# First piece of weights in two halves, compression's weights loaded at another place, residual pairs inside priority blocks, two squares left to TensorE

## The chip, the cores and the metric

One core of one Trainium2 chip runs the whole program; the other cores are idle. The metric is the device time of one execution in microseconds (us). TensorE (PE) multiplies, VectorE (DVE) and ScalarE (ACT) do the elementwise work, SyncE (SP) issues the transfers from memory, GpSimd (POOL) does almost nothing.

## The reference

256 positions of width 1024 in float32 go through a first part of two layers and a second part of two layers. Each layer of the first part has three kinds of attention side by side (one of them with a compressed branch: blocks of 32 keys and values go through a small network with the weights `cw1` and `cw2`), cross attention to a memory of 256 rows, and a gated feed-forward with a short convolution. The second part has a retention layer and a convolution layer, each followed by a feed-forward, with scales, shifts and gates that come from a condition vector:

```python
hx = hx + g1 * yx                                   # yx: retention or convolution mixer
fx = modulate(rms_norm_2(hx, norm_ffn[i]), sh2, sc2)
hx = hx + g2 * swiglu(fx, ffn_w1[i], ffn_w3[i], ffn_w2[i])
...
return rms_norm_2(hx, final_norm)
```

The kernel returns the 256 x 1024 result of the last norm.

## The kernel before, in words

**Numbers in three products.** Every float32 weight `w` is split into a coarse part `wh` (a cast on ScalarE, line 378) and a rest `wl` (a subtraction on VectorE, line 379), every activation likewise into `xh` and `xl`. A product is three matmuls on TensorE: `wh,xh`, `wh,xl`, `wl,xh` (helper `mm`, line 297).

**Weights.** `Stream` (line 344) brings the weights in pieces of 128 x 1024 numbers (512 KB; some are a little smaller) in the order in which the program asks for them: SP issues the transfer into one of five `raw` buffers, ScalarE and VectorE split it into one of four pairs `wh`, `wl`. A buffer pair comes free with the last matmul that reads it.

**Activations.** `X` holds the 8 tiles (k = 0 to 7) of 128 channels by 256 positions. Two tiles are a pair. `residual_pair` (line 750) adds a finished bank `o` to a pair of X, `split_gain` makes `xh` and `xl` of its two tiles for the next layer, and `Norm.pair` squares the pair on ScalarE and adds the squares into `ss` on VectorE. `Norm.totals` adds the two halves and lets PE sum over the channels; `rsqrt` makes the norm's factor of it (`rx` to `ry` in the rows). A factor is put to use after the matmuls of the next layer, so the next layer's matmuls start with `xh` and `xl` and not with the norm. With `late`, the last pair's square isn't added into `ss`: PE sums it by itself.

**Residuals of the second part.** `residual` (line 1580) calls `residual_pair(os_(p), p, ...)` for the four pairs. It is called four times: after the retention, after the first feed-forward, after the convolution mixer, after the second feed-forward. In three of them `os_(p)` returns a bank that is finished already (`accs[p]`). At the convolution's output `os_(p)` is `fm(bxs)` (line 487): it asks for two pieces of weights and issues the 48 matmuls of that pair. In the rows of before the four banks there are `mm_16337`, `mm_16406`, `mm_16476`, `mm_16546`.

**Memory and compression.** In each layer of the first part `mem_pair` (line 791) splits the memory's rows from the tile `memx`, loaded in two halves into one buffer with the tag `big4`. The same buffer then takes the compression's first weights in two halves (`load_w1`, line 800; the tile is `w1`, in the trace `w`), called in `compress` (line 895) just before the matmuls that read each half.

**What sets the order.** A scheduler orders each engine's instructions by a priority, which is the place in the program, and by when their inputs are there in its own reckoning. `tc.high_priority(offset=n)` moves what stands in the block ahead by n places and sets the place back on leaving the block to where it was on entering it. `PRIO` is 300.

Of the kernel before, what the change touches and what calls it, by code (L numbers as in the profile page):

```python
# [10 lines left out]
F32 = mybir.dt.float32  # L11
# [3 lines left out]
AF = mybir.ActivationFunctionType  # L15
ALU = mybir.AluOpType
# [258 lines left out]
def tile_two_blocks(ctx, tc, aps, out):  # L275
    nc = tc.nc
    W, X_IN, MEM_IN, CTX_IN = aps["w"], aps["x"], aps["mem"], aps["ctx"]
# [24 lines left out]
    def tt(out, a, b, op):  # L302
        V.tensor_tensor(out=out, in0=a, in1=b, op=op)  # L303
# [10 lines left out]
    def act(out, a, func, scale=1.0, bias=None, accum_out=None):  # L314
        kw = {}
        if bias is not None:
            kw["bias"] = bias
        if accum_out is not None:
            kw["accum_out"] = accum_out
        A.activation(out=out, in_=a, func=func, scale=scale, **kw)  # L320
# [23 lines left out]
    class Stream:  # L344
# [12 lines left out]
        def dma(s):  # L357
            i = s.n_dma
            if i >= len(_PLAN) or i >= s.n_split + s.nraw:
                return  # L360
            t = wraw_p.tile([128, 1024], F32, tag="raw", name="raw", bufs=s.nraw)
            b, first = i // _PER, (i // _PER) * _PER
            n = _SIZES[i]
            o = sum(_SIZES[first:i]) * 128
            nc.sync.dma_start(out=t[:, :n], in_=W[b][o:o + 128 * n].rearrange("(p n) -> p n", p=128))
            s.raw[i] = t, n
            s.n_dma += 1

        def split(s):
            i = s.n_split  # L370
            if i >= s.n_dma:
                return False
            pools, bufs, ids = s.rings[int(i < s.until and i % 2)]
            if len(ids) >= bufs and ids[-bufs] >= (s.n_get - 1 if s.hold is None else s.hold):
                return False
            t, n = s.raw.pop(i)
            h, l = (p.tile([128, 1024], F32R, tag=a, name=a, bufs=bufs, at=128) for p, a in zip(pools, ("wh", "wl")))
            act(h[:, :n], t[:, :n], AF.Copy)
            tt(l[:, :n], t[:, :n], h[:, :n].bitcast(F32), ALU.subtract)
            ids.append(i)  # L380
            s.parts[i] = h, l, n
            s.n_split += 1
            s.dma()
            return True
# [156 lines left out]
    PRIO = 300  # L541
# [9 lines left out]
    class Norm:  # L551


        def __init__(s, gains=None, tags=("a0", "a1"), late=False):
            s.ss, s.last = None, None
            s.gains = gains
            s.tags = tags
            s.late = late
            s.prio = PRIO

        def pair(s, p, src=None, ps=None):
            src = X if src is None else src
            ps = p if ps is None else ps
            tag = "ss" if s.ss is None else "sq"
            sq = rot_p.tile([128, 2, T], F32, tag=tag, name=tag)
            if s.gains is None:
                act(sq, src[:, 2 * ps:2 * ps + 2, :], AF.Square)
            else:
                for e in range(2):
                    k = 2 * p + e  # L570
                    act(sq[:, e, :], src[:, k, :], AF.Square, scale=s.gains[:, k:k + 1])
            if s.ss is None:
                s.ss = sq
            elif p == 3 and s.late:
                s.last = sq
            else:
                tt(s.ss, s.ss, sq, ALU.add)

# [4 lines left out]

        def totals(s):
            s.ps = bank(s.tags[0])
            parts = [s.ss] if s.last is None else [s.ss, s.last]
            for a, part in enumerate(parts):
                tt(part[:, 0, :], part[:, 0, :], part[:, 1, :], ALU.add)
                for t in range(2):
                    mm(s.ps[:, t:t + 1], part[:, 0, t * 128:(t + 1) * 128], ones[:, 0:1], start=a == t == 0, stop=True)  # L590
# [65 lines left out]
    nrm, xs = Norm(), xs_tiles()  # L656
# [93 lines left out]
    def residual_pair(o, p, gain, nrm, xs, g=None):  # L750
        xv = X[:, 2 * p:2 * p + 2, :]
        if g is None:
            tt(xv, xv, o.rearrange("p (n t) -> p n t", n=2), ALU.add)
        else:
            for e in range(2):
                k = 2 * p + e
                stt(X[:, k, :], o[:, e * T:(e + 1) * T], g[:, k:k + 1], X[:, k, :], ALU.mult, ALU.add)
        if gain is not None:
            for k in (2 * p, 2 * p + 1):
                split_gain(xs, X, k, gain)  # L760
        nrm.pair(p)
# [15 lines left out]
    def layer(i, xs, nrm, last_gain, background=None, second=None):  # L777
        with ExitStack() as es:
# [10 lines left out]
            memx = {}  # L789

            def mem_pair(p):
                if p % 2 == 0:
                    memx["t"] = cp.tile([128, 4, T], F32, tag="big4", name="memx")
                    nc.sync.dma_start(out=memx["t"], in_=MEM_IN[:, 2 * p:2 * p + 4, :])
                for k in (2 * p, 2 * p + 1):
                    split_gain(mxs, memx["t"], k, vec(("norm_mem", i)), k - 2 * (p // 2) * 2)
                if i == 0:
                    mnrm.pair(p, memx["t"], p % 2)

            def load_w1(e):  # L800
                t = cp.tile([128, 8, 128], F32, tag="big4", name="w1")
                nc.sync.dma_start(out=t, in_=aps["cw1"][i].rearrange("p (j c) -> p j c", j=16)[:, 8 * e:8 * e + 8, :])
                return t
# [24 lines left out]
            o = run(tok(xs, 512, 4))  # L828
# [6 lines left out]
            o = run(tok(xs, 412, 4))  # L835
# [59 lines left out]
            def compress():  # L895
                KB = cp.tile([128, 16, 2, 2, 15], F32, tag="KB", name="KB")
                for e in range(2):
                    pe = vec(("pe_k" if e == 0 else "pe_v", i))
                    for g in range(2):
                        for half in range(2):  # L900
                            src = KC2[:, e, g, half * 16:half * 16 + 240].rearrange("p (n j two) -> p j n two", j=8, two=2)[:, :, :, 0]
                            tt(KB[:, half * 8:half * 8 + 8, e, g, :], src,
                               pe[:, half * 8:half * 8 + 8].unsqueeze(2).to_broadcast([128, 8, 15]), ALU.add)
                yield
                hp = bank()
                for j in range(16):
                    if j % 8 == 0:
                        w1 = load_w1(j // 8)
                    mm(hp[:, 0:60], w1[:, j % 8, :], KB[:, j].rearrange("p e g n -> p (e g n)"), start=j == 0, stop=j == 15)
                H = cp.tile([128, 32], F32, tag="H", name="H")[:, :30]  # L910
                E = cp.tile([128, 32], F32, tag="E", name="E")[:, :30]
                for e in range(2):
                    q = slice(64 * e, 64 * e + 64)
                    A.copy(out=H[q], in_=hp[q, 30 * e:30 * e + 30])
                    tsc(E[q], hp[q, 30 * e:30 * e + 30], -1.0, ALU.mult, 80.0, ALU.min)
                act(E, E, AF.Exp)
                tsc(E, E, 1.0, ALU.add)
                V.reciprocal(out=E, in_=E)
                tt(H, H, E, ALU.mult)
                HV = cp.tile([128, 4, 2, 16], F32, tag="HV", name="HV")  # L920
                V.memset(HV, 0.0)
                V.tensor_copy(out=HV[64:128, :, :, 0:15], in_=H[64:128].rearrange("p (g n) -> p g n", g=2).unsqueeze(1).to_broadcast([64, 4, 2, 15]))
                yield
                p = bank()
                mm(p[:, 0:30], w2[0:64, :], H[0:64, :], start=True, stop=True)
                V.memset(KCT, 0.0)
                A.copy(out=KCT[0:64, 0:15], in_=p[0:64, 0:15])
                A.copy(out=KCT[64:128, 16:31], in_=p[64:128, 15:30])
                p = bank()
                mm(p[:, 0:64], HV[64:128].rearrange("p r g n -> p (r g n)"), w2[64:128, 0:64], start=True, stop=True)  # L930
                vb = cp.tile([128, 64], F32, tag="vb", name="vb")
                A.copy(out=vb, in_=p[:, 0:64])
                tt(VBD, vb.unsqueeze(1).to_broadcast([128, 8, 64]), cst("bd").unsqueeze(2).to_broadcast([128, 8, 64]), ALU.mult)
                done.add("compress")
# [644 lines left out]

    def residual(os_, gate, after, xs):  # L1580

        nrm = Norm(late=after is None, tags=("a2", "a3"))
        for p in range(4):
            residual_pair(os_(p), p, after and GS[:, after[0], after[1], :], nrm, xs, g=gate)
        return nrm, xs

    nrm, xs = residual(lambda p: accs[p], PAR[:, 0, 16:24], (0, 1), xs)
# [163 lines left out]
```

## Time and profile before

| | us |
|---|---|
| three executions | 1511.64, 1520.8, 1525.02 |
| their median | 1520.8 |
| the profiled execution | 1516.69 |
| its span in the trace | 1514.9 |
| busy: TensorE, VectorE, ScalarE | 1482.2, 1186.5, 810.1 |
| mean granted clock of TensorE, share of full speed | 0.993 |
| moved by transfers | 292.95 MB, mean 193 GB/s |

Times in the rows count from the span's start. In a row of a timeline the first number is the start, the second the time from the start to the end of the instructions that the row groups, then come engine, line, operation, output and inputs, tile shape and count; a bracket at the end gives the engine's idle time before it and what ended that. Matmuls overlap in the engine, so a row of 0.28 us and a next row that starts 0.11 us later are one stream without a gap. Line 297 is the matmul helper, 303 and 312 are VectorE helpers, 320 is ScalarE's; the tiles tell which work it is.

### The profile page before, as it was taken

Reading aid. Unit: us, or ns where it says so; the run is one execution under the profiler, and the core shown is the slowest. Engines: PE = TensorE matmul, PEld = TensorE weight load, DVE = VectorE, ACT = ScalarE, POOL = GpSimd, SP = SyncE. Lnnn points to the kernel's source line nnn. Section 1 sums busy time; section 2 is a strip of 40 time slices with the busy share of each in tenths; the row PEclk is TensorE's granted clock in tenths of the full one; section 3 lists DMA queues with packets and bytes.
Section 4 is the critical chain, followed back from the end, with each engine's and each line's share of the span. In section 5 each row is a group of like instructions: output and inputs, shape, how many; then the busy total and the mean of one; then the engine's idle time right before and its main releaser. Section 6 shows DMA issues by size and latency. Waiting matters only on the chain.

```text
span 1514.9 us, 30232 instructions
## 1 busy us (share of the span) xinstructions
PE 1482.2 (98%) x12130; PEld 1420.1 (94%) x12130; DVE 1186.5 (78%) x2285; ACT 810.1 (53%) x1437; POOL 0.2 (0%) x4
## 2 busy tenths in 40 slices
PE   8899999999999999999999999999999999999997
PEld 6877999999886889999999999999999999999997
DVE  7677789998898889998795766668977788885555
ACT  6455676565755566665543434335544465664443
POOL 0000000000000000000000000000000000000000
PEclk9999999999999999999999999999999999999999
DMA  8621456776562366676544556465788865656661
GB/s 296 219 84 31 147 172 204 255 237 213 188 230 71 117 204 218 207 259 230 177 159 168 196 169 209 150 196 182 263 303 292 287 200 185 187 179 194 198 192 68
DMA packets 81212, 292.95 MB, mean 193 GB/s; under 512 B 9136, under 2 KB 9136, under 8 KB 80944
## 3 DMA queue, kind: packets, MB, share of 16 engines
q1 hardware_dynamic: 81072, 291.03, 58.4%
q8 instruction: 95, 1.56, 0.4%
q14 instruction: 45, 0.37, 0.1%
HBM read 289.94 MB, written 1.05 MB: 192 GB/s over the span
## 4 chain that ended last, share of the span: by engine, by line
PE 90%; DVE 4%; DMA 3%; ACT 2%; issue 1%; SPq 0%; DVEq 0%; ACTq 0%
PE mm L297 60%; PE a L297 28%; PE a L742 1%; DMA raw<-in_w_dram 1%; DVE xl L312 1%; DVE wl L303 1%; DVE ss L303 1%; DMA memx<-in_mem_dram 1%; ACT wh L320 1%; DMA w<-in_cw_dram 1%; DVE X L303 0%; PE a L617 0%; ACT xh L320 0%; ACT PT L743 0%; ACT y L320 0%
## 5 line engine op out<-in xcount | busy, mean ns | idle before, releaser
L303 DVE TENSOR_TENSOR wl<-raw,wh 128x1024 fp32r<-128x1024 f32 (+2 forms) x440 | 533.3, 1216 | 177.7 <-ACT wh L320 174.6
L320 ACT ACTIVATE wh<-raw 128x1024 fp32r<-128x1024 f32 (+2 forms) x440 | 459.6, 1049 | 351.5 <-PE mm L297 182.7
L297 PE MATMUL mm<-xh,wh 128*128 128x256 f32 (+1 forms) x2064 | 575.4, 280 | 2.6 <-ACT fj L320 2.6
L297 PE MATMUL mm<-xl,wh 128*128 128x256 f32 x2064 | 577.0, 280 | 0.0
L297 PE MATMUL mm<-xh,wl 128*128 128x256 f32 (+1 forms) x2064 | 575.6, 279 | 0.0
L297 PEld LDWEIGHTS mm<-xh,wh 128*128 128x128 f32 x2064 | 389.4, 189 | 3.6 <-ACT fj L320 3.0
L297 PEld LDWEIGHTS mm<-xl,wh 128*128 128x128 f32 x2064 | 390.7, 189 | 1.3 <-DVE xl L312 0.6
L297 PEld LDWEIGHTS mm<-xh,wl 128*128 128x128 f32 x2064 | 389.4, 189 | 0.0
L312 DVE SCALAR_TENSOR_TENSOR adaj<-adaw,CC 128x1024 bf16<-128x1024 f32 x112 | 136.7, 1221 | 0.1
L297 PE MATMUL mm<-wh,xh 128*128 128x256 f32 (+3 forms) x384 | 119.0, 311 | 7.0 <-ACT wh L320 7.0
L297 PE MATMUL mm<-wl,xh 128*128 128x256 f32 (+3 forms) x384 | 119.2, 311 | 0.0
L297 PE MATMUL mm<-wh,xl 128*128 128x256 f32 (+3 forms) x384 | 118.6, 309 | 0.0
L297 PE MATMUL a<-sh,wl 128*128 128x256 f32 x352 | 98.0, 279 | 0.0
L297 PE MATMUL a<-sh,wh 128*128 128x256 f32 x352 | 98.0, 278 | 0.0
L297 PE MATMUL a<-sl,wh 128*128 128x256 f32 x352 | 98.0, 278 | 0.0
L297 PE MATMUL a<-fsl,wh 128*128 128x256 f32 x352 | 96.9, 276 | 0.0
L297 PE MATMUL a<-fsh,wh 128*128 128x256 f32 x352 | 96.7, 276 | 0.0
L297 PE MATMUL a<-fsh,wl 128*128 128x256 f32 x352 | 96.6, 276 | 0.0
L297 PEld LDWEIGHTS mm<-wh,xh 128*128 128x128 f32 x384 | 72.6, 189 | 10.8 <-ACT wh L320 7.0
L312 DVE SCALAR_TENSOR_TENSOR y<-U,VEC,y 128x256 f32<-128x256 f32 x176 | 74.4, 484 | 2.8 <-ACT y L320 2.7
L297 PEld LDWEIGHTS mm<-wl,xh 128*128 128x128 f32 x384 | 72.6, 189 | 4.1 <-DVE wl L303 1.1
L297 PEld LDWEIGHTS mm<-wh,xl 128*128 128x128 f32 x384 | 72.7, 189 | 2.5
(308 smaller groups left out, 2418.0 us busy)
## 6 DMA issues: line engine op xcount, KB each, us to landing
raw<-in_w_dram SPq DMA_DIRECT2D x424, 512.0 KB, 4.1
adaw<-in_ada_dram SPq DMA_DIRECT2D x96, 512.0 KB, 4.5
raw<-in_w_dram SPq DMA_DIRECT2D x8, 416.0 KB, 3.9
raw<-in_w_dram SPq DMA_DIRECT2D x8, 384.0 KB, 4.3
memx<-in_mem_dram SPq DMA_DIRECT2D x4, 512.0 KB, 5.6
w<-in_cw_dram SPq DMA_DIRECT2D x4, 512.0 KB, 4.6
dec<-in_dec_dram SPq DMA_DIRECT2D x4, 512.0 KB, 4.2
X<-in_x_dram SPq DMA_DIRECT2D x4, 256.0 KB, 5.1
```

The source lines that it names most:

```text
L297: nc.tensor.matmul(out, lhsT, rhs, start=start, stop=stop, skip_group_check=True)
L303: V.tensor_tensor(out=out, in0=a, in1=b, op=op)
L312: return V.scalar_tensor_tensor(out=out, in0=a, scalar=s, in1=b, op0=op0, op1=op1, accum_out=accum_out)
L320: A.activation(out=out, in_=a, func=func, scale=scale, **kw)
L742: nc.tensor.transpose(pt[:, b:b + 128], Ps[u][:, h, kt * 128:(kt + 1) * 128], ident)
```

## The change

Four edits. The first piece of weights is transferred, cast and subtracted as two halves of 512 columns. The first half of the compression's weights is asked for at the end of the last `mem_pair` and no longer in `compress`. In `residual`, each pair stands in a priority block, with an offset of 300 in the last call and of 0 in the others. In the last call the squares of the last two pairs, and no longer of the last one alone, are left out of `ss` and summed on TensorE.

```diff
+            for c in s.parts_of(i, n):
+                nc.sync.dma_start(out=t[:, c], in_=src[:, c])
...
+        def parts_of(s, i, n):
+
+            return [slice(0, n)] if i else [slice(0, n // 2), slice(n // 2, n)]
...
-            act(h[:, :n], t[:, :n], AF.Copy)
-            tt(l[:, :n], t[:, :n], h[:, :n].bitcast(F32), ALU.subtract)
+            for c in s.parts_of(i, n):
+                act(h[:, c], t[:, c], AF.Copy)
+                tt(l[:, c], t[:, c], h[:, c].bitcast(F32), ALU.subtract)
...
-            elif p == 3 and s.late:
-                s.last = sq
+            elif p >= 4 - s.late:
+                s.last.append(sq)
...
-            parts = [s.ss] if s.last is None else [s.ss, s.last]
-            for a, part in enumerate(parts):
+            for a, part in enumerate([s.ss] + s.last):
...
+                if p == 3:
+                    memx["w1"] = load_w1(0)
...
-                        w1 = load_w1(j // 8)
+                        w1 = load_w1(1) if j else memx["w1"]
...
-        nrm = Norm(late=after is None, tags=("a2", "a3"))
+        nrm = Norm(late=0 if after else 2, tags=("a2", "a3"))
         for p in range(4):
-            residual_pair(os_(p), p, after and GS[:, after[0], after[1], :], nrm, xs, g=gate)
+            with tc.high_priority(offset=0 if after else PRIO):
+                residual_pair(os_(p), p, after and GS[:, after[0], after[1], :], nrm, xs, g=gate)
```

What moves at the convolution's output, on PE. Before, at the change from the first pair's bank to the second's (`xh_15384` is the mixer's result):

```order
L297 MATMUL mm_16337<-xh_15384,wh_16267 128x256
L297 MATMUL mm_16337<-xl_15385,wh_16267 128x256
L297 MATMUL mm_16337<-xh_15384,wl_16268 128x256
L297 MATMUL mm_16406<-xh_15384,wl_16339 128x256
L297 MATMUL mm_16406<-xh_15384,wh_16338 128x256
L297 MATMUL mm_16406<-xl_15385,wh_16338 128x256
```

The bank of a pair is finished before the next one's matmuls go on. After the change, the last of the 192 matmuls of the four pairs (`mm_16340`, `mm_16409`, `mm_16479`, `mm_16549`) and the first of the feed-forward behind them:

```order
L297 MATMUL mm_16340<-xl_15388,wh_16270 128x256
L297 MATMUL mm_16549<-xl_15388,wh_16510 128x256
L297 MATMUL mm_16409<-xh_15387,wl_16372 128x256
L297 MATMUL mm_16340<-xh_15387,wl_16271 128x256
L297 MATMUL mm_16479<-xh_15387,wl_16441 128x256
L297 MATMUL mm_16549<-xh_15387,wl_16511 128x256
L297 MATMUL mm_16624<-xh_16332,wh_16550 128x258
L297 MATMUL mm_16625<-xh_16332,wh_16550 128x258
L297 MATMUL mm_16707<-xh_16332,wh_16626 128x258
L297 MATMUL mm_16708<-xh_16332,wh_16626 128x258
L297 MATMUL mm_16624<-xl_16333,wh_16550 128x256
```

The four banks are worked on in turn and end one right after the other, and the fifth matmul behind them is the first that reads `xl`.

DVE at the same place, before, over the last two pairs (PAR is the gate, GS the next layer's gain):

```order
L312 SCALAR_TENSOR_TENSOR X_83<-mm_16476,PAR_127,X_83 128x256 x2
L303 TENSOR_TENSOR wl_16578<-raw_16411,wh_16577 128x1024
L312 SCALAR_TENSOR_TENSOR xl_16330<-X_83,GS_128,xh_16329 128x256 x2
L303 TENSOR_TENSOR ss_16404<-ss_16404,sq_16543 128x512
L303 TENSOR_TENSOR wl_16624<-raw_16441,wh_16623 128x1024
L312 SCALAR_TENSOR_TENSOR X_83<-mm_16546,PAR_127,X_83 128x256 x2
L303 TENSOR_TENSOR wl_16675<-raw_16481,wh_16674 128x1024
L312 SCALAR_TENSOR_TENSOR xl_16330<-X_83,GS_128,xh_16329 128x256 x2
```

After:

```order
L312 SCALAR_TENSOR_TENSOR X_83<-mm_16340,PAR_128,X_83 128x256
L303 TENSOR_TENSOR wl_16551<-raw_16375,wh_16550 128x1024
L303 TENSOR_TENSOR wl_16581<-raw_16414,wh_16580 128x1024
L303 TENSOR_TENSOR wl_16627<-raw_16444,wh_16626 128x1024
L303 TENSOR_TENSOR wl_16678<-raw_16484,wh_16677 128x1024
L312 SCALAR_TENSOR_TENSOR X_83<-mm_16479,PAR_128,X_83 128x256
L312 SCALAR_TENSOR_TENSOR X_83<-mm_16549,PAR_128,X_83 128x256
L312 SCALAR_TENSOR_TENSOR X_83<-mm_16409,PAR_128,X_83 128x256
L312 SCALAR_TENSOR_TENSOR X_83<-mm_16479,PAR_128,X_83 128x256
L312 SCALAR_TENSOR_TENSOR X_83<-mm_16549,PAR_128,X_83 128x256
L312 SCALAR_TENSOR_TENSOR X_83<-mm_16340,PAR_128,X_83 128x256
L312 SCALAR_TENSOR_TENSOR xl_16333<-X_83,GS_129,xh_16332 128x256 x8
```

The first row stands behind one more update of X (from `mm_16409`). The updates, the splits of weights and the `xl` that were spread over four pairs now stand in one row behind the four banks, and the eight `xl` (in the order k = 4, 0, 2, 6, 3, 1, 5, 7) are last.

DVE at the end of the program, before:

```order
L312 SCALAR_TENSOR_TENSOR X_83<-a2_16957,PAR_127,X_83 128x256
L303 TENSOR_TENSOR ss_18846<-ss_18846,sq_18850 128x512
L312 SCALAR_TENSOR_TENSOR X_83<-a2_16957,PAR_127,X_83 128x256
L312 SCALAR_TENSOR_TENSOR X_83<-a3_16958,PAR_127,X_83 128x256 x2
L303 TENSOR_TENSOR ss_18846<-ss_18846,sq_18855 128x512
L303 TENSOR_TENSOR ss_18846<-ss_18846 128x256
L303 TENSOR_TENSOR sq_18860<-sq_18860 128x256
```

After:

```order
L312 SCALAR_TENSOR_TENSOR X_83<-a2_16960,PAR_128,X_83 128x256 x2
L303 TENSOR_TENSOR ss_18849<-ss_18849,sq_18853 128x512
L312 SCALAR_TENSOR_TENSOR X_83<-a3_16961,PAR_128,X_83 128x256 x2
L303 TENSOR_TENSOR ss_18849<-ss_18849 128x256
L303 TENSOR_TENSOR sq_18858<-sq_18858 128x256
L303 TENSOR_TENSOR sq_18862<-sq_18862 128x256
```

One addition of 512 columns is gone, one of 256 columns is new, and both updates of the third pair stand together.

## Rows read from the trace of the kernel before

**Rows 1.** The page: span, and TensorE's busy time, share and instructions
```profile
span 1514.9 us, 30232 instructions
...
PE 1482.2 (98%) x12130; PEld 1420.1 (94%) x12130; DVE 1186.5 (78%) x2285; ACT 810.1 (53%) x1437; POOL 0.2 (0%) x4
```

**Rows 2.** Waits of PE: what for, us in total, times, longest
```profile
PE mm L297 <- DMA w<-in_cw_dram: 3.4, 2, 2.8
...
PE mm L297 <- ACT fj L320: 2.6, 2, 2.0
```

**Rows 3.** Stretches: length, busy time of each engine, PE clock, DMA share
```profile
1035.00:1065.00 30.00, 28.02 (x228) 27.47 (x227) 28.01 (x57) 16.48 (x29) 0.00 (x0) 0.98 0.70 238
...
1225.00:1260.00 35.00, 34.98 (x293) 34.67 (x293) 32.28 (x70) 22.98 (x53) 0.00 (x0) 1.00 0.57 182
...
1300.00:1330.00 30.00, 29.83 (x256) 29.35 (x255) 24.97 (x48) 16.58 (x26) 0.00 (x0) 1.00 0.62 192
1330.00:1500.00 170.00, 170.00 (x1494) 170.00 (x1493) 100.26 (x132) 83.03 (x134) 0.00 (x0) 1.00 0.56 174
```

**Rows 4.** Timeline of PE, convolution's output, 21 steps apart
```profile
1318.27 0.28 PE L297 MATMUL mm<-xh,wl 128*128 128x256 f32 x1
...
1320.65 0.28 PE L297 MATMUL mm<-xh,wl 128*128 128x256 f32 x1
```

**Rows 5.** Timeline of DVE, convolution's output, the last pair
```profile
1320.97 0.88 DVE L312 SCALAR_TENSOR_TENSOR X<-mm,PAR,X 128x256 f32<-128x256 f32 x2 [0.46 <-PE mm L297]
1322.00 1.23 DVE L303 TENSOR_TENSOR wl<-raw,wh 128x1024 fp32r<-128x1024 f32 x1 [0.15 <-ACT wh L320]
1323.14 0.88 DVE L312 SCALAR_TENSOR_TENSOR xl<-X,GS,xh 128x256 fp32r<-128x256 f32 x2
```

**Rows 6.** Timeline of ACT, the cast of weights at the same place
```profile
1320.90 1.06 ACT L320 ACTIVATE wh<-raw 128x1024 fp32r<-128x1024 f32 x1 [1.65 <-PE mm L297]
```

**Rows 7.** Timeline of all engines, the start
```profile
1.17 0.42 SPq L645 DMA_DIRECT2D X<-in_x_dram  x1
1.64 0.42 SPq L365 DMA_DIRECT2D raw<-in_w_dram  x1
...
4.09 0.91 ACT L320 ACTIVATE xh<-X,VEC 128x256 fp32r<-128x256 f32 x2 [2.07 <-DMA X<-in_x_dram]
...
5.93 1.06 ACT L320 ACTIVATE wh<-raw 128x1024 fp32r<-128x1024 f32 x1 [0.42 <-DMA raw<-in_w_dram]
...
7.04 1.22 PE L297 MATMUL mm<-wh,xh 128*128 128x512 f32 x2 [7.04 <-ACT wh L320]
...
8.17 2.46 DVE L312 SCALAR_TENSOR_TENSOR xl<-X,VEC,xh 128x256 fp32r<-128x256 f32 x6
...
13.21 0.19 PEld L297 LDWEIGHTS mm<-wl,xh 128*128 128x128 f32 x1 [0.30 <-DVE wl L303]
```

**Rows 8.** Timeline of PE around the compression of the first layer
```profile
59.99 1.89 PE L297 MATMUL mm<-KB,w 128*128 128x60 f32 x16
...
67.97 3.67 PE L297 MATMUL mm<-KB,w 128*128 128x60 f32 x16 [2.82 <-DMA w<-in_cw_dram]
...
73.90 0.39 PE L297 MATMUL a<-xh,wh 128*128 128x256 f32 x1
...
74.24 0.28 PE L297 MATMUL a<-xh,wl 128*128 128x256 f32 x1
```

**Rows 9.** Timeline of PE after the retention's residual
```profile
1062.43 0.39 PE L297 MATMUL mm<-xh,wh 128*128 128x258 f32 x1 [1.98 <-ACT fj L320]
```

**Rows 10.** Timeline of SP, the issues of the compression's weights
```profile
39.63 0.33 SPq L802 DMA_DIRECT2D w<-in_cw_dram  x1
...
61.92 0.33 SPq L802 DMA_DIRECT2D w<-in_cw_dram  x1
```

**Rows 11.** Timeline of ACT and PE, the end
```profile
1504.32 0.61 ACT L320 ACTIVATE sq<-X 128x512 f32<-128x512 f32 x1
...
1505.25 0.60 PE L297 MATMUL a<-CST,ss 128*128 128x1 f32 x4 [2.36 <-DVE ss L303]
```

More of the change, by code (lines that the diff above doesn't have):

```diff
@@ L364, in dma @@
             o = sum(_SIZES[first:i]) * 128
-            nc.sync.dma_start(out=t[:, :n], in_=W[b][o:o + 128 * n].rearrange("(p n) -> p n", p=128))
+            src = W[b][o:o + 128 * n].rearrange("(p n) -> p n", p=128)
+            for c in s.parts_of(i, n):
+                nc.sync.dma_start(out=t[:, c], in_=src[:, c])
             s.raw[i] = t, n
             s.n_dma += 1
+        def parts_of(s, i, n):
+            return [slice(0, n)] if i else [slice(0, n // 2), slice(n // 2, n)]
         def split(s):
@@ L554, in __init__ @@
         def __init__(s, gains=None, tags=("a0", "a1"), late=False):
-            s.ss, s.last = None, None
+            s.ss, s.last = None, []
             s.gains = gains
```

## The prediction, as it went on record

> **What bounds the kernel now.** I read the page first, then the table of waits, then a table of stretches, and only then single rows. The page says that TensorE (PE) is busy for 1482.2 of 1514.9 us [rows 1]; all its idle time together is 33 us, so no edit can win more than that, and any wait that the edit puts in front of PE is paid in full unless PE was going to wait there anyway. The waits say where PE still waits: once for the second half of the compression's weights (2.8 of the 3.4 us in two waits), once for `fj` (2.0 of 2.6 us) [rows 2]. The stretches say where something could hide: from 1330 to 1500 us PE is busy for 170.00 of 170 us, so nothing that is late before 1330 is given back after it; from 1035 to 1065 us VectorE (DVE) is busy for 28.01 of 30 us and sets the pace; from 1300 to 1330 us PE has only 0.17 us idle and DVE still has 5 us [rows 3].
>
> **The change, part by part.** The diff has four edits, and one of them reaches further than its name: `with tc.high_priority(offset=...)` now stands around every pair of every call of `residual`, with offset 0 in three calls of four. The block sets the order back on leaving it, so all four pairs of a call, and what the program writes after them, start from one and the same place in the order. In the calls that only read finished banks (after the retention, after the first feed-forward) this moves rows of DVE. In the call at the convolution's output `os_(p)` itself makes the matmuls inside the block, so the matmuls of four pairs become equals, and the order rows show what the scheduler then does.
>
> *Convolution's output.* Before, each pair is 48 matmuls in a row. They come every 0.1133 us (21 steps from 1318.27 to 1320.65) [rows 4], so a pair is ready each 5.4 us, and its two updates of X (0.88 us for both), one split of weights (`wl`, 1.23 us, next one 1.14 us later) and two `xl` (0.88 us) run on DVE under the matmuls of the next pair [rows 5]. After, all four banks end within the last four of the 192 matmuls. The wh buffers are four, and the last pieces of the four pairs hold all of them to the end, so the four splits for the feed-forward (`wh_16550` to `wh_16677`) also start only then. Call the end of the 192nd matmul T0 (1320.9 before). DVE's order is then fixed: two updates (0.88), four `wl` (4 x 1.14 = 4.56; ScalarE's four `wh` of 1.06 us each run one ahead of them [rows 6]), six updates (6 x 0.44 = 2.64), and two `xl`, of which the second is the one for k=0 that PE's fifth matmul reads (0.88). That is T0 + 8.96. PE does four `xh` matmuls in that time, 0.45 us of work. It loses 8.96 - 0.45 = 8.5 us, less 0.1 because the first updates may start three matmuls before T0: **8.4 us**. The bounds are 7.0 (updates and `xl` at 0.40 us each, the pitch at which the six `xl` of the start run [rows 7], and 0.5 us more of overlap) and 9.5 (0.1 us more at each hand-over between engines).
>
> Behind such a wait PE does not run at full speed. After the wait of 2.82 us at 67.97 the 16 matmuls with 60 columns took 3.67 us where the first 16 took 1.89, and the ones with 256 columns ran at 0.41 us until 73.90 and at 0.28 from 74.24 [rows 8]: half the clock for 5.9 us, that is 2.95 us lost. After the wait of 1.98 us at 1062.43 only one matmul is longer (0.39) [rows 9], so a wait of 2 us costs nothing more. The new wait is three times the longer of these two, so I take **2.9 us**; bounds 0 (as after 1.98 us) and 4.0 (the four matmuls that trickle in during the wait keep the clock low for longer).
>
> Inside the 192 matmuls there is a second price. Eight pieces of weights pass through four buffers, and three pieces (`wh_16410`, `wh_16480`, `wh_16510`) reuse a buffer whose last reader is about 11 matmuls before their own first reader: 11 x 0.1133 = 1.25 us for a cast of 1.06 us and two hand-overs. I take 0.13 us each, **0.4 us**, bounds 0 and 3 x 1.2 = 3.6 (a whole `wl` exposed each time). No wait behind this place exists that would swallow it [rows 3]. The term is 8.4 + 2.9 + 0.4 = **+11.7 us**, bounds +7 and +17.
>
> The Trainium skill has a rule that speaks against this order: its page "Perfetto Trace Analysis", section "Matmuls", wants independent groups of matmuls to rotate through banks, so that the emptying of one overlaps the matmuls of the next. By that rule alone the new order would cost the emptying of the banks, and the sum would be about +3.5; the rows of DVE's order put the four `wl` in front of it, which gives the larger sum.
>
> *Retention's residual (1040 us).* PE is fed there by the same DVE rows; after the edit DVE does all eight updates of X (0.44 us each) before the first `xl`, where before `xl` came after three, so `xl` is 5 x 0.44 = 2.2 us late and PE, which has four `xh` matmuls and the rest of the old banks to do, waits about 1 to 2 us more near 1043. But PE waits 1.98 us at 1062.43 for `fj`, behind a DVE that is busy for 28.01 of these 30 us [rows 3, 9]: what DVE has to do is the same, so most of it is swallowed there. I take **+0.5 us**, bounds -0.3 and +2.5. *First feed-forward's residual*: PE has 0.02 us idle in the 35 us around it [rows 3] and the updates only change places with two `xl`; **0**, bounds -0.3 and +0.5.
>
> *First piece in halves.* The whole piece (512 KB) is issued at 1.64 and its cast starts at 5.93, 4.29 us later; X's first 256 KB are issued at 1.17 and read at 4.09, 2.92 us later [rows 7]. So the first half is there between 1.64 + 2.92 = 4.56 and 5.9, I take 5.0; with half a cast PE starts at about 5.5 instead of 7.04. But at 13.21 PE waits 0.30 us for `wl` of the second piece, which DVE makes behind six `xl` (from 8.17), and these read X's other parts [rows 7]; neither is moved by the halves; the second transfer and one more cast and subtraction are new on those engines. So PE's early start ends in a longer wait at 13.2. Gain **-0.4 us**, bounds 0 and -1.6.
>
> *Compression's weights.* The first half is issued at 39.63 already, right when its buffer comes free, and used at 59.99 [rows 8, 10]: writing it earlier gains nothing. The second half waits for the first eight matmuls to free that buffer (issued 61.92, 6.05 us before 67.97), and PE's order around it is the same before and after: **0**, bounds 0 and +0.5 (SP issues one 768-column piece ahead of the other transfers around 35 us).
>
> *The end.* The last pair's square starts at 1504.32, its halves are added and PE reads the sums at 1505.25 [rows 11]. Now the third pair's square is left to PE as well: DVE saves one addition between the updates and the sums, PE gets two more matmuls of one column. But ScalarE does three `fin` between the squares of the third and the last pair, so the last square hardly starts sooner. **-0.15 us**, bounds 0 and -0.6.
>
> **The sum.** -0.4 + 0 + 0.5 + 0 + 11.7 - 0.15 = +11.65 us. The profiled execution took 1516.7 us (span 1514.9 and 1.8 around it), 4.1 below the median of 1520.8. On its own time the sum gives 1528.3, on the median 1532.4; I give the middle, **1530 us**.
>
> **The rivals.**
>
> *A, dearer: slower by over 1%.* The hand-overs of weights inside the 192 matmuls expose a whole `wl` each (+3.2 over my term) and the retention's wait isn't swallowed (+1.5): one mechanism, DVE as the bottleneck wherever the pairs of a residual come together. It decides if the cast needs more than the 1.25 us that the buffer gives it. For it: the margin is 0.2 us. Against it: DVE has 5 us free in 1300 to 1330 [rows 3]. Sum +16.4, 1535.
>
> *B, only the emptying of the banks shows*: 8 updates x 0.44 = 3.5 us, if the splits of weights were done in the idle time before T0, and PE's clock stays up. Against it: the order rows put `wl_16551` behind the first updates, and its buffer is free only at T0. Sum +3.4, 1522. This is what the skill's page "Perfetto Trace Analysis", section "Matmuls", would have it cost.
>
> *C, the compression's wait goes away too*: 2.82 us and 2.95 us of slow clock [rows 8] if the second half were issued earlier. Against it: its buffer is freed by PE's own matmuls, whose order stands. Sum +5.9, 1524.
>
> *D, not slower*: the updates at the convolution come early enough for PE because the scheduler meant them to, nothing is lost there, and the start and the end gain what they were bounded by (-2.2): 1516.
>
> **How the numbers follow.** Forecast (+8 to +14) 0.62; A 0.18; B 0.10; C 0.06; D 0.04. One per cent is 15.2 us, about what a measurement of this kernel can tell from no change. Over that lies A and the upper edge of the forecast's case: 0.2; faster by over 1% needs D and a disturbance of the runs, whose own spread is 13 us: 0.03; the rest, 0.77, is within 1%. The range takes in C and B's upper part and A: 1518 to 1539.
>
> **What would show it.** In the profile of the changed kernel PE should have one new wait of 6 to 8 us near 1321, released by DVE's `xl` (and shorter ones by DVE's updates just before), with half the clock for about 6 us behind it; the first matmul should stand at about 5.5 us, and a wait for `wl` longer than 0.30 us near 13; the wait of 2.8 us for `w` should be there still; PE's busy time should be the same outside the slow stretches. I am wrong if PE runs through 1321 without a wait over 3 us, if that wait is behind something other than DVE, or if a second wait of that size shows elsewhere.

## The result and the profile after

The changed kernel took 1521.5 us (median of 21 executions, 1513.8 to 1534.1), the kernel before 1512.7 us (21 executions, 1505.9 to 1525.0). The ratio is 1.006, interval 1.0038 to 1.0083: 6 to 13 us slower, some 9 us. The profiled execution of the changed kernel has a span of 1515.8 us, 0.9 us more than that of before; why two spans lie closer together than the medians is told in the last section.

The page of the changed kernel, span and busy time:

```profile
span 1515.8 us, 30244 instructions
...
PE 1479.3 (98%) x12134; PEld 1416.0 (93%) x12134; DVE 1185.1 (78%) x2286; ACT 809.2 (53%) x1438; POOL 0.2 (0%) x4
```

Its waits of PE, what for, us in total, times, longest (answers to [rows 2]):

```profile
PE mm L297 <- DVE X L312: 6.4, 1, 6.4
...
PE mm L297 <- DMA w<-in_cw_dram: 2.8, 2, 2.3
...
PE mm L297 <- DVE xl L312: 1.7, 3, 1.2
...
PE mm L297 <- ACT fj L320: 1.0, 2, 0.7
```

The first row is new, and by far the longest wait of the program behind the start. The wait for `w` is still there. Of the two waits for `fj` the first has shrunk from 1.98 us [rows 9] to 0.38 (below); the second, 0.67 us at 1082.70 before, is still 0.67. One for `xl` of 1.2 us has come ahead of them.

```profile
1053.64 0.39 PE L297 MATMUL mm<-xh,wh 128*128 128x258 f32 x1 [0.38 <-ACT fj L320]
```

Its stretches (columns as in [rows 3]):

```profile
1035.00:1065.00 30.00, 29.33 (x233) 28.72 (x232) 27.36 (x58) 16.78 (x36) 0.00 (x0) 0.95 0.68 212
...
1300.00:1340.00 40.00, 33.32 (x251) 32.13 (x250) 25.93 (x50) 18.31 (x33) 0.00 (x0) 0.87 0.42 141
1340.00:1500.00 160.00, 160.00 (x1410) 160.00 (x1409) 93.53 (x122) 77.25 (x121) 0.00 (x0) 1.00 0.56 175
```

From 1300 to 1340 us PE is idle for 6.7 us, and its mean granted clock is 0.87 of full speed; before, PE had 0.17 us idle in 30 there. From 1340 on it is busy without a gap, as before: what was lost stays lost. The granted clock fell to half (1.2 of 2.4 GHz) at 1314.58, 2.5 us after PE's last matmul had ended, and rose at 1324.82; the stretch between:

```profile
1314.58:1324.82 10.24, 6.15 (x25) 5.64 (x26) 10.07 (x21) 6.08 (x13) 0.00 (x0) 0.50 0.56 206
```

PE at the convolution's output, after (timeline; answers to [rows 4]):

```profile
1311.41 0.62 PE L297 MATMUL mm<-xh,wl 128*128 128x256 f32 x4
1318.46 1.66 PE L297 MATMUL mm<-xh,wh 128*128 128x258 f32 x4 [6.44 <-DVE X L312]
1320.33 0.58 PE L297 MATMUL mm<-xl,wh 128*128 128x256 f32 x1 [0.21 <-DVE xl L312]
...
1324.58 0.40 PE L297 MATMUL mm<-xh,wl 128*128 128x258 f32 x1
1324.79 0.31 PE L297 MATMUL mm<-xh,wh 128*128 128x258 f32 x1
```

DVE at the same place (timeline; answers to [rows 5]):

```profile
1311.72 0.88 DVE L312 SCALAR_TENSOR_TENSOR X<-mm,PAR,X 128x256 f32<-128x256 f32 x2 [5.13 <-PE mm L297]
1312.51 4.62 DVE L303 TENSOR_TENSOR wl<-raw,wh 128x1024 fp32r<-128x1024 f32 x4
1317.05 2.44 DVE L312 SCALAR_TENSOR_TENSOR X<-mm,PAR,X 128x256 f32<-128x256 f32 x6
1319.40 3.25 DVE L312 SCALAR_TENSOR_TENSOR xl<-X,GS,xh 128x256 fp32r<-128x256 f32 x8
```

This is the row that the order promised: DVE is idle for 5.1 us under the last matmuls, since no bank is finished, and then does two updates, four splits, six updates and two `xl` while PE waits (six more `xl` follow). The last four of the 192 matmuls start at 1311.41, the first `xl` matmul at 1320.33, and the matmuls run at half the clock until 1324.79 (0.215 us from one to the next, 0.12 behind that).

To set the traces side by side I took the start of instructions that each kernel has once per place, read to 0.1 us, and subtracted. Against before, the changed kernel's trace is 0.3 us ahead at 17 us, 1.2 at 60, 3.0 at 96, 4.8 at 629, 9.5 at 737, 11.2 at 1041, 9.8 at 1089 and still 9.8 at 1301; at 1334 it is 0.8 us behind, and 0.9 at the end. So the convolution's output costs 10.6 us in this pair of traces, give or take 0.1.

### The profile page after: what moved, and what is told of

Read it like the earlier page. It is cut to its first block, busy times and chain, and to the rows that moved or that the text cites. A ratio compares the mean times of both kernels' runs of the same rounds, so it can differ in the third digit from the quotient of the medians.

```text
span 1515.8 us, 30244 instructions
## 1 busy us (share of the span) xinstructions
PE 1479.3 (98%) x12134; PEld 1416.0 (93%) x12134; DVE 1185.1 (78%) x2286; ACT 809.2 (53%) x1438; POOL 0.2 (0%) x4
## 3 DMA queue, kind: packets, MB, share of 16 engines
q8 instruction: 95, 1.56, 0.4%
## 5 line engine op out<-in xcount | busy, mean ns | idle before, releaser
L303 DVE TENSOR_TENSOR wl<-raw,wh 128x1024 fp32r<-128x1024 f32 (+3 forms) x441 | 532.4, 1211 | 183.3 <-ACT wh L320 182.4
L320 ACT ACTIVATE wh<-raw 128x1024 fp32r<-128x1024 f32 (+3 forms) x441 | 458.7, 1047 | 345.4 <-PE mm L297 188.1
L297 PEld LDWEIGHTS mm<-wh,xh 128*128 128x128 f32 x384 | 72.5, 189 | 10.2 <-ACT wh L320 6.6
```

The lines of the kernel that those rows point to most:

```text
L297: nc.tensor.matmul(out, lhsT, rhs, start=start, stop=stop, skip_group_check=True)
```

## The experiments

Times of an edit below are of two kinds. The ratio of medians has an interval of 0.2 to 0.4% (3 to 6 us), so it tells the large terms. For the small ones I use the same difference of starts over a short stretch of two traces. halves_only and tail_only have one execution each and no ratio.

**tail_block_only: the changed kernel without its three blocks of offset 0.**

```diff
-            with tc.high_priority(offset=0 if after else PRIO):
-                residual_pair(os_(p), p, after and GS[:, after[0], after[1], :], nrm, xs, g=gate)
+            if after:
+                residual_pair(os_(p), p, GS[:, after[0], after[1], :], nrm, xs, g=gate)
+            else:
+                with tc.high_priority(offset=PRIO):
+                    residual_pair(os_(p), p, None, nrm, xs, g=gate)
```

> The changed kernel without the three blocks of offset 0: the halves, the compression's weights, the two squares and the block of offset 300 at the end stay. Theory (the loss comes from the blocks of offset 0, above all at the convolution's output): PE's wait of 6.4 us near 1312 is gone, the matmuls of the four pairs stand one bank after the other again, and the time is 0 to 3 us under the kernel before, that is some 9 to 12 us under the changed one; ratio to before 0.998 to 1.000. Rival (the loss comes from the other edits, and the wait at the convolution only takes the place of one that would be there anyway): ratio stays near 1.006.

Ratio to before 0.9981, interval 0.9952 to 1.0011 (1512.8 us against 1513.1). The stretch at the convolution reads as before:

```profile
1290.00:1330.00 40.00, 39.86 (x335) 39.36 (x334) 31.86 (x59) 21.62 (x40) 0.00 (x0) 1.00 0.58 182
```

PE has 0.14 us idle in 40 us. The loss is gone, and with it the sign: the other three edits are worth nothing that this measurement can tell from no change. The theory holds.

**blocks_only: the kernel before with nothing but the three blocks of offset 0.**

```diff
+            if after:
+                with tc.high_priority(offset=0):
+                    residual_pair(os_(p), p, GS[:, after[0], after[1], :], nrm, xs, g=gate)
+            else:
+                residual_pair(os_(p), p, None, nrm, xs, g=gate)
```

> The kernel before with nothing but blocks of offset 0 around the pairs of the three residuals. Theory: the whole loss of the change and a little more, since the small gains of the other edits are missing: +10 to +13 us, ratio 1.007 to 1.009, with one wait of 6 to 7 us for an update of X at about 1321 and half the clock for 6 us behind it. Rival: within 3 us of before.

Ratio 1.0104, interval 1.0067 to 1.0141 (1532.1 us): the whole loss, and probably more than I expected (10 to 13 us against an interval of 10 to 21). The trace below accounts for 11 us, the lower end of it; I can't place the rest. The wait stands where it should:

```profile
1329.36 1.67 PE L297 MATMUL mm<-xh,wh 128*128 128x258 f32 x4 [6.42 <-DVE X L312]
1331.23 0.58 PE L297 MATMUL mm<-xl,wh 128*128 128x256 f32 x1 [0.20 <-DVE xl L312]
```

Against before, its trace is 0.9 us behind at 1301 and 12.0 behind at 1334: 11.1 us in this one place, and nothing is given back after it (12.0 at 1502).

**blocks_banks_outside: the same, but the bank's matmuls stand ahead of the block.**

```diff
+            o = os_(p)
+            if after:
+                with tc.high_priority(offset=0):
+                    residual_pair(o, p, GS[:, after[0], after[1], :], nrm, xs, g=gate)
```

> The kernel before with a block of offset 0 around residual_pair alone; os_(p), and with it the convolution's 192 matmuls, stands ahead of the block. Theory (it is the matmuls inside the block that cost): PE at the convolution's output reads as before, without a wait over 1 us; the retention's and the first feed-forward's rows of DVE still move, worth 0 to +2 us; ratio 1.000 to 1.002. Rival (the updates of X, moved ahead of the splits of weights, are what costs): +8 us or more, with a wait at about 1321 as in the changed kernel.

Ratio 1.0028, interval 0.9994 to 1.0062, so of the 1.0104 most is gone. At the convolution nothing is left of the loss (4.2 us behind before at 1301, 4.3 at 1334); PE has 0.17 us idle in 30, as before [rows 3]:

```profile
1304.00:1334.00 30.00, 29.83 (x256) 29.34 (x256) 25.17 (x48) 16.84 (x30) 0.00 (x0) 1.00 0.62 193
```

At the retention's residual the two waits remain:

```profile
1046.03 0.51 PE L297 MATMUL mm<-xh,wh 128*128 128x258 f32 x2 [1.03 <-ACT wh L320]
1047.69 0.38 PE L297 MATMUL mm<-xl,wh 128*128 128x256 f32 x1 [1.15 <-DVE xl L312]
```

They make 2.2 us, the wait for `fj` behind them shrinks from 1.98 to 0.38, and what is left in the differences of starts is 1.5 us (2.7 us behind at 1041, 4.2 at 1301). So it is the matmuls inside the block (with the requests for their weights, which moved out with them) that cost at the convolution, and not the place of the updates as such; the rival that blamed the updates falls.

**second_half_other_buffer: tail_block_only, and the compression's second half in another buffer, asked for earlier.**

```diff
-                t = cp.tile([128, 8, 128], F32, tag="big4", name="w1")
+                t = cp.tile([128, 8, 128], F32, tag=("big4", "KC2")[e], name="w1")
...
+                second = load_w1(1)
                 yield
...
-                        w1 = load_w1(1) if j else memx["w1"]
+                        w1 = memx["w1"] if j < 8 else second
```

> The kernel tail_block_only with the second half of the compression's weights in the buffer of KC2, which DVE reads for the last time at about 57.7 us, and asked for right there; the first half stays where the change put it. Theory: issued at about 57 and landed by 63, it is there before PE asks at 65, so the wait of 2.3 to 2.8 us is gone, and with it the slow clock behind it in the first layer (2.9 us at most), and 0.6 us in the second layer: 3 to 6 us under tail_block_only, ratio to before 0.995 to 0.998. Rival (the transfer is late for lack of bandwidth, or the slow clock has another cause, the 60-column matmuls themselves): less than 1.5 us under tail_block_only.

A miss: ratio 1.0054, interval 1.0025 to 1.0082, some 8 us over tail_block_only. The transfer did start 5 us earlier, at 56.60, but PE waits 2.14 us for it, against 2.82 in before's trace and 0.90 in tail_block_only's:

```profile
58.68 1.89 PE L297 MATMUL mm<-KB,w 128*128 128x60 f32 x16
62.70 3.31 PE L297 MATMUL mm<-KB,w 128*128 128x60 f32 x16 [2.14 <-DMA w<-in_cw_dram]
...
69.75 0.36 PE L297 MATMUL a<-xl,wh 128*128 128x256 f32 x1
```

The scheduler reckoned the second half to be there and put its 8 products right behind the first 8, where 31 others had stood between the two groups; the transfer took 6.0 us to land and PE waited again, with the slow clock behind it until 69.9. The differences of starts show 3.8 us less gained in the first layer (60 to 152 us) than in tail_block_only and 1.6 us more lost in the second (from 405 to 517 us). The rest of the 8 us I can't place.

**second_half_later_reader: the same with a break between the two groups of matmuls.**

```diff
                         w1 = memx["w1"] if j < 8 else second
+                        if j:
+                            yield
```

> The kernel second_half_other_buffer with a break in the compression's program between the matmuls of the two halves, so that other matmuls stand between them again (44 instead of 8 from the first reader of one half to the first reader of the other). Theory (the wait stayed because the scheduler, with the second half loaded earlier, put its readers right behind the first ones): issued at about 56.6 and there at 62.7, the second half is now early for readers at about 64; no wait for `w` over 0.5 us in either layer, and the first layer is 1 to 5 us shorter at 100 us than in tail_block_only's trace, depending on whether the slow clock behind the 60-column matmuls goes too. Rival (the slow clock comes from the short matmuls themselves): the wait goes, the matmuls behind them still take 0.41 us, gain under 2 us. Ratio to before 0.995 to 1.000.

Now the second half is early, and nothing waits or slows down:

```profile
61.12 1.89 PE L297 MATMUL mm<-KB,w 128*128 128x60 f32 x16
...
66.62 1.89 PE L297 MATMUL mm<-KB,w 128*128 128x60 f32 x16
```

The same 16 matmuls take 1.89 us where they took 3.67 [rows 8], and PE's clock is 1.00 from 62 to 80 us:

```profile
62.00:80.00 18.00, 17.97 (x147) 15.41 (x146) 13.43 (x45) 7.83 (x29) 0.00 (x0) 1.00 0.46 157
```

So the short matmuls by themselves didn't bring the clock down here. That the wait does is not shown by this alone: the next run has the wait and keeps the clock. In the first layer this kernel gains 4.1 us against before from 60 to 152 us, tail_block_only 3.3. But the ratio is 0.9992, interval 0.9960 to 1.0023, no better than tail_block_only: the order of the second layer's attention moved too, and from 405 to 517 the kernel loses 1.1 us against before (tail_block_only 0.6), though the wait for `w` is gone there as well. One wait less is not one wait's time less as long as a scheduler reorders the rest.

**first_half_early_only: the request for the first half moved, nothing else.** The compiled order is that of before on every engine, row for row.

> The kernel before with nothing but the request for the compression's first half moved to the end of the last mem_pair. The compiled order is that of before on every engine, row for row, so this is the same program but for its source. Theory: ratio 1.000 within its interval, issue of the first half at 39 to 40 us, the wait for the second half still 1 to 3 us. Rival: faster by 0.2% or more. What it differs by from 1 also says how far two sets of runs of one program can lie apart here.

Ratio 1.0008, interval 0.9976 to 1.0040. The wait for the second half is 2.47 us. This part of the change did nothing that the ratio can tell, and one program against itself differs by 0.08% here, inside its interval. In this trace the same wait is followed by no slow clock: the 16 matmuls take 2.00 us, and the granted clock is 1.00 from 62 to 80 us, where before's trace has 3.67 us [rows 8] at half clock.

```profile
68.06 2.00 PE L297 MATMUL mm<-KB,w 128*128 128x60 f32 x16 [2.47 <-DMA w<-in_cw_dram]
```

**halves_only: the first piece in halves, nothing else.**

> The kernel before with nothing but the first piece in two halves. Theory: PE starts at 5.2 to 5.6 us, waits 0.5 us or a little more for `wl` near 13, and is 0.2 to 0.6 us ahead of before at 21 us; rows of 40 to 60 us move as in the changed kernel. Rival: the whole 1.6 us of the earlier start is still there at 21 us.

PE at the start (timeline; the rows of before are in [rows 7]):

```profile
5.48 0.80 PE L297 MATMUL mm<-wh,xh 128*128 128x512 f32 x1 [5.48 <-ACT wh L320]
...
11.58 0.74 PE L297 MATMUL mm<-wh,xh 128*128 128x512 f32 x2 [1.26 <-ACT wh L320]
...
12.84 0.51 PE L297 MATMUL mm<-wl,xh 128*128 128x512 f32 x1 [0.52 <-DVE wl L303]
```

PE starts 1.56 us sooner and pays most of it back in two waits for the second piece, 1.26 and 0.52 us, where before had one of 0.30; at 17 us it is 0.4 us ahead. (The clock rose to full at 9.1 us, in before at 12.7, so the waits aren't the whole account.) The rival of the whole 1.6 us falls.

**tail_only: two squares left to TensorE and the block of offset 300, nothing else.**

> The kernel before with nothing but the end: two squares left to TensorE and the block of offset 300. Theory: from the last matmul of the second feed-forward to the end of the program 0 to 0.3 us shorter than before (there 1502.6 to 1514.9). Rival: 0.6 us shorter or more, for one addition of VectorE is gone from the path.

The norm's factor starts 3.37 us behind the start of the last large matmul; before it was 3.73 (1506.34 behind 1502.61):

```profile
1497.45 0.42 DVE L303 TENSOR_TENSOR sq<-sq 128x256 f32<-128x256 f32 x1 [0.37 <-ACT sq L320]
1498.57 0.16 DVE L309 TENSOR_SCALAR rx<-a 128x2 f32<-128x2 f32 x1 [0.70 <-PE a L297]
```

0.36 us, a little over what I expected, and neither of the two cases. In the changed kernel's trace the factor starts 3.78 us behind, for the eight small matmuls took 1.67 us and not 1.27: the granted clock had fallen to half at 1505.7, while they ran; in tail_only it fell at 1499.1, behind them, and in before at 1507.7.

```profile
1505.47 1.67 PE L297 MATMUL a<-CST,sq 128*128 128x1 f32 x8
```

Traces of like clock tell what the edit is worth: where the clock fell before the sums were done, the old end takes 4.29 us (halves_only), 4.48 (blocks_only) and 4.54 (blocks_banks_outside), the new one 3.61 to 3.78 (tail_block_only, second_half_later_reader, the changed kernel).

## Why the prediction was right, point by point

**The large term held in place and size.** The prediction put 11.7 us at the convolution's output; the traces show 10.6 in the changed kernel and 11.1 in blocks_only, and blocks_banks_outside shows that it hangs on the matmuls inside the block. Its three parts, worked out for the changed kernel:

| part | predicted | measured | how |
|---|---|---|---|
| wait of PE | 8.4 | 8.0 | would-be start 1311.85 to first `xl` matmul 1320.33, less 4 matmuls of 0.12 |
| slow clock | 2.9 | 2.1 | 20 matmuls from 1320.33 to 1324.79 take 4.46 us; at 0.119 they take 2.4 |
| hand-overs inside the 192 matmuls | 0.4 | 0.8 | first to last start 22.94 us (1288.81 to 1311.75), before 22.12 (1298.54 to 1320.65) |

The would-be start is the time at which the first matmul behind the 192 would follow them without a wait, 0.11 us behind the start of the last one; the three parts make 10.9 us, 0.3 more than the differences of starts. The hand-overs came at three places, as predicted, but each cost 0.4 us and not 0.13; before has one place of 0.4 us there too, which leaves 0.8. The slow clock was over-priced in one step: I took the whole 5.9 us of half clock from [rows 8] as time in which PE would work. The clock was at half for 10.2 us here (1314.58 to 1324.82), but 3.9 us of it passed while PE was idle, and 1.9 us while it did four matmuls and waited for `xl`; that time is already in the wait.

**A reading that was wrong.** "A wait of 2 us costs nothing more" was read from too few rows behind 1062.43. In the same trace the clock falls 1.5 us later, and the matmuls take 0.42 us each from 1064.0 to 1067.4:

```profile
1064.00:1067.40 3.40, 3.40 (x19) 3.40 (x18) 2.53 (x7) 0.87 (x1) 0.00 (x0) 0.50 0.90 296
```

So that row was no ground for a lower bound of 0 on the slow clock. Nor is a wait of this length always followed by half clock: seven traces have the wait of 1.98 us, in four of them the clock falls behind it (before, second_half_later_reader, halves_only, tail_only), in three it stays at full (tail_block_only, second_half_other_buffer, first_half_early_only). That the new wait would be followed by half clock held: both traces that have it (the changed kernel, blocks_only) show 10.2 us of half clock.

**The waits that were named.** PE's wait is 6.44 us, "6 to 8 us" said the prediction; it is put down to an update of X and not to `xl`, since the four `xh` matmuls come between, and the shorter one for `xl` stands behind it and not ahead. The wait for `w` stayed (2.35 us), the first matmul stands at 5.40, the wait for `wl` near 13 grew to 0.53; a wait for `wh` of 0.65 us came with it that I had not named.

**The retention's residual** was priced at 0.5 us and is worth 1.4 us in the changed kernel, 1.5 in blocks_banks_outside: inside the bounds. The waits of 1.03 and 1.15 us are there, and of them the smaller wait for `fj` gives back 1.6 (1.98 to 0.38), "most of it" as I had counted. That leaves 0.6 us, near the prediction; the other 0.8 I can't place. More than either hangs on the clock: in these two traces it falls to half behind the new waits (0.95 of full speed from 1035 to 1065 in the changed kernel). blocks_only has the same two waits, to the hundredth, but keeps the clock,

```profile
1040.00:1070.00 30.00, 28.89 (x236) 28.14 (x237) 28.47 (x62) 18.00 (x38) 0.00 (x0) 1.00 0.67 214
```

and there the place costs nothing against before (4.5 us ahead of it at 1041, 4.5 at 1077). Before's own trace has half clock behind the wait for `fj`, so 1.4 us is the price where both fall. The first feed-forward's residual is worth 0, as predicted (9.8 us ahead on both sides).

**The start** gained 0.3 us (0.4 in halves_only), predicted 0.4. **The compression's first half** gained nothing, as the order had shown. **The end** gained 0.36 us where the clock stayed up, predicted 0.15; against before's trace the changed kernel's gained nothing, because its clock fell sooner.

**The rivals.** A (dearer, over 1%) would have needed whole splits exposed inside the 192 matmuls: the hand-overs cost 0.8 us more than before together. B (only the emptying of the banks, 3.5 us) is ruled out by the row of DVE: 4.6 us of splits lie inside the wait. The rule of the Trainium skill, "Perfetto Trace Analysis", section "Matmuls", that independent groups should rotate through banks so that the emptying of one overlaps the matmuls of the next, is right about the direction; the trace agrees that the banks which end together here aren't emptied under the next matmuls (DVE idle for 5.13 us, then PE for 6.44). C falls because the wait for `w` stayed, D because of the new wait.

**The level.** 1530 us was predicted, 1521.5 measured. The change accounts for 2.6 us of the difference (11.65 predicted, about 9 measured); the other 6 come from the base: I had four executions of before, whose middle was 1518.7 us, and 21 give a median of 1512.7. By the time alone B (1522) and C (1524) were nearer than the forecast; only the traces tell them apart.

## What to carry to other kernels

A priority block that restores its place on leaving makes equals of all that is written in a loop of such blocks: look what the calls inside it issue, above all when an argument is a function that issues matmuls. In this kernel, four accumulations that end one after the other left three of four evacuations under matmuls, four that end together left none, and the buffers that their last operands held added the next stage's preparation to the wait. When a transfer is made earlier, look in the order whether its reader moved up with it.

## What the runs showed of the hardware that was not expected

**Two rates of the same matmuls at the same granted clock.** In long stretches without a gap PE starts either about 170 or about 177 of the 256-column products in 20 us, 0.1178 or 0.1134 us each, and keeps one rate for the whole stretch. (The counts in rows of stretches, as below, are two or three higher, since they take in the matmuls that overlap an edge.) The same instructions of the first feed-forward of the first part, with PE clock 0.99 both times; kernel before, then the changed one:

```profile
580.00:700.00 120.00, 118.55 (x998) 118.38 (x997) 113.65 (x201) 78.05 (x121) 0.00 (x0) 0.99 0.69 227
```

```profile
580.00:700.00 120.00, 118.44 (x1029) 118.26 (x1028) 117.22 (x209) 78.84 (x123) 0.00 (x0) 0.99 0.70 227
```

The changed kernel does 31 matmuls more in the same busy time. Over the ten traces of this study (one execution each), matmuls started per 20 us in the four long stretches of the program, away from their gaps:

| kernel | 240 to 380 | 560 to 700 | 1080 to 1200 | 1360 to 1500 |
|---|---|---|---|---|
| before | 177 | 170 | 177 | 177 |
| after | 177 | 177 | 177 | 177 |
| tail_block_only | 170 | 170 | 177 | 177 |
| blocks_only | 177 | 170 | 170 | 177 |
| blocks_banks_outside | 170 | 170 | 177 | 177 |
| second_half_other_buffer | 177 | 170 | 170 | 177 |
| second_half_later_reader | 170 | 177 | 170 | 177 |
| first_half_early_only | 177 | 170 | 177 | 177 |
| halves_only | 177 | 177 | 170 | 177 |
| tail_only | 177 | 177 | 177 | 177 |

One slow stretch of 140 us costs 140 x 7/177 = 5.5 us, so three of them would make up most of a spread of 19 us between executions of before; no trace here has more than two, and the other executions weren't traced. It is also why two single traces can't be compared by their spans: before's profiled execution had one slow stretch (its trace loses 4.7 us to that of the changed kernel between 629 and 737 us, where both run the same rows), the changed kernel's had none. first_half_early_only, tail_only and before have the same matmuls in the same order in the first three stretches and show both rates in the second (170, 177, 170), so the order alone doesn't fix the rate. What sets it, and whether a kernel's order makes one rate more likely, stays open; I tried nothing on it, and it may be the part of second_half_other_buffer's loss that I couldn't place.

**The transfer of 512 KB for the compression** (the second half, first layer) landed between 3.9 us (halves_only) and 6.0 us (before) after its issue in the eight traces that ask for it at the old place, and the wait of PE for it ran from 0.76 to 2.82 us. Whoever prices such a wait by one trace has one draw of it.
